# Padding in front of two groups of SBUF tiles, so that matmul operands start at multiples of 2 KB

## The chip, the core and the metric

One NeuronCore of a Trainium2 chip runs the whole program. The metric is the time of one execution on the device in microseconds (us). TensorE (PE in the profile) has two clock levels, 1.2 and 2.4 GHz; the profile gives the granted clock as a share of the upper one. Below, "SBUF address" means the byte offset inside one partition; all 128 partitions of a tile lie at the same offset.

## The reference

One decoder layer over 1,024 tokens of width 1,024, in float32:

```python
h = rmsnorm(x);  proj = h @ w_in                                  # 1024 x 7168
y_a = (a_b * causal_dwconv(a_c * a_x, conv_a_w)) @ w_out_a          # 3 taps
u   = causal_dwconv(c_val * sigmoid(c_gate), conv_b_w) + conv_b_b   # 31 taps
y_b = silu(layernorm(u)) @ w_out_b
x   = x + (sigmoid(gate_a) * y_a + sigmoid(gate_b) * y_b) @ w_o
x   = x + hierarchical_moe(rmsnorm(x))      # 32 experts, top group, top 2 in it, 1024->512->1024
x   = x + sigmoid(rmsnorm(x) @ w_ple_gate) * (p @ w_ple_proj)
return rmsnorm(x)
```

## The kernel before, in words

**Matmul form.** The projections are done in the type float32r (one pass of TensorE). To keep float32 accuracy, both operands are split into a high and a low part (`split`, lines 94 to 96: ACT writes the high part at L95, DVE the low part at L96), and three products are added: high by high, high by low, low by high. Each of them is one instruction on 128 contraction rows, 128 output rows and 512 columns; the trace calls it MATMUL 128x512 f32. The stationary operand (128x128, 512 bytes per partition) is loaded by a LDWEIGHTS of its own for every matmul; the moving operand is 512 columns, 2,048 bytes per partition.

**Stages.**
1. Start (0 to about 43 us): x is normed and transposed into `hT`, the high and low halves of the eight tiles `a0` to `a7` (L143).
2. Loop `s1` (L224 to L253, eight rounds `cb`): five projections of `hT` with chunks of `w_in`. A projection (`proj`, L162) loads a 1024x128 chunk of weights into `wraw` from the SP queue, splits it into the ring tiles `wh` and `wl` (`wchunk`, L146), and issues 48 matmuls at L159: 8 k by 3 products by 2 column halves. DVE also runs the 31-tap convolution here: 30 instructions per round at L251.
3. Block `s2` (L314 to L393): the gates, `w_out_a` and `w_out_b`, again by `proj` and L159; the moving operand is `hT` (tiles a) or `Y` (tiles b), the stationary one again `wh` or `wl`.
4. `w_o` (L419): here the stationary operand is `M`, 128-column slices of the tiles a, and the moving one is the split `w_o` in the tiles b. The routing of the tokens runs beside it.
5. The experts (L830, L857, transposes L794 and L843): plain float32 matmuls. Weights stream from HBM through the same tiles a and b and four more (`c0` to `c3`) with the SP queue.
6. The last stage: the gate matmul with `w_ple_gate`, split as in stage 2 (L1204 for seven blocks of rows, L1271 for the last one). The moving operand is `GW`, in tiles a and b; the stationary one `XW`, 128-column slices of the tiles `xts` and `ys`, filled after transposes (L106).

**Where the tiles lie.** A pool takes a contiguous piece of SBUF when it is opened and places its tiles in it in the order of their first use, each rounded up to a multiple of 32 bytes. `const` comes first, then `big` (the tiles a and b, 8,192 bytes each), then `wrawp` and `wring`, later `mpw` and `mp`. The first tile of `wring` is `vecs`, then `cw`, then the ring `wh`, `wl`. The order of the work is set by the tile framework up to stage 3 and by hand from `w_o` on (`manual_schedule`). The functions that matter here are `layer_kernel`, which holds the pools, and `token_stat`, a helper of stage 3:

Of the kernel before, what the change touches and what calls it, by code (L numbers as in the profile page):

```python
# [10 lines left out]
F32 = mybir.dt.float32  # L11
# [10 lines left out]
T = 1024  # L22
# [41 lines left out]
def layer_kernel(ctx: ExitStack, tc: tile.TileContext, A, out, dbg=None):  # L64
# [3 lines left out]
    const = ctx.enter_context(tc.tile_pool(name="const", bufs=1))  # L68
# [11 lines left out]
    def tpsum():  # L80
        return psum.tile([128, 512], F32, name="tp", bufs=2)
# [4 lines left out]
    def flat(t):  # L86
        return t.rearrange("p a b -> p (a b)")
# [6 lines left out]
    def split(h, l, src):  # L94
        nc.scalar.activation(h, src, AF.Copy)  # L95
        nc.vector.tensor_tensor(l, src, h.bitcast(F32), op=OP.subtract)  # L96

    def rstd_of(dst, ms):

        nc.gpsimd.tensor_scalar(dst, ms, EPS, None, op0=OP.add)  # L100
        nc.gpsimd.tensor_tensor(dst, dst, mhalf[:, :dst.shape[1]], op=OP.pow)
# [17 lines left out]
    def vec(i, k):  # L119
        return vecs[:, i * 8 + k:i * 8 + k + 1]  # L120
# [9 lines left out]
    iota_s = const.tile([1, NE], F32, name="iota_s")  # L130
    ovi = const.tile([1, 2 * NOV + 1], I32, name="ovi")

    big = ctx.enter_context(tc.tile_pool(name="big", bufs=1))
    mix = ctx.enter_context(ExitStack())
    front = mix.enter_context(ExitStack())
    wrawp = front.enter_context(tc.tile_pool(name="wrawp", bufs=3))
    wring = front.enter_context(tc.tile_pool(name="wring", bufs=2))

    vecs = wring.tile([128, NV * 8], F32, name="vecs", bufs=1)
    cw = wring.tile([128, 8, 34], F32, name="cw", bufs=1)  # L140
    bufA = [big.tile([128, 2048], F32R, name=f"a{i}") for i in range(8)]
    bufB = [big.tile([128, 2048], F32R, name=f"b{i}") for i in range(8)]
    hT = [[a[:, i * T:(i + 1) * T] for a in bufA] for i in range(2)]  # L143
# [18 lines left out]
    def proj(src, c0, act):  # L162
        w = wchunk(src, c0)
        ps = mpsum()
        for hf in range(2):
            proj_half(w, ps, act, hf)
        return flat(ps)
# [56 lines left out]
    with tc.tile_pool(name="s1", bufs=2) as s1:  # L224
        for cb in range(8):
            pg = proj(w_in, 4 * D + cb * 128, hT) if cb else flat(fps[0])
            sg = s1.tile([128, T], F32, name="tmp", bufs=2)
            nc.scalar.activation(sg, pg, AF.Sigmoid)
            pv = proj(w_in, 3 * D + cb * 128, hT) if cb else flat(fps[1])
            u = s1.tile([128, KB - 1 + T], F32, name="u")  # L230
            nc.gpsimd.memset(u[:, :KB - 1], 0.0)
            nc.vector.tensor_tensor(u[:, KB - 1:], pv, sg, op=OP.mult)
            acc = s1.tile([128, T], F32, name="acc")
            nc.scalar.activation(acc, u[:, :T], AF.Identity, scale=cw[:, cb, 0:1], bias=vec(V_CB, cb))  # L234
            pc = proj(w_in, D + cb * 128, hT)
            cx = s1.tile([128, T], F32, name="tmp", bufs=2)
            nc.scalar.activation(cx, pc, AF.Copy)
            px = proj(w_in, 2 * D + cb * 128, hT)
            m = s1.tile([128, 2 + T], F32, name="m", bufs=1)
            nc.gpsimd.memset(m[:, :2], 0.0)  # L240
            nc.vector.tensor_tensor(m[:, 2:], px, cx, op=OP.mult)
            c3 = s1.tile([128, T], F32, name="c3", bufs=1)
            nc.scalar.activation(c3, m[:, :T], AF.Copy, scale=cw[:, cb, KB:KB + 1])
            for t in (1, 2):
                nc.vector.scalar_tensor_tensor(c3, m[:, t:t + T], cw[:, cb, KB + t:KB + t + 1], c3,
                                               op0=OP.mult, op1=OP.add)
            pb = proj(w_in, cb * 128, hT)
            nc.vector.tensor_tensor(c3, pb, c3, op=OP.mult)
            split(Y[0][cb], Y[1][cb], c3)
            for t in range(1, KB):  # L250
                nc.vector.scalar_tensor_tensor(acc, u[:, t:t + T], cw[:, cb, t:t + 1], acc,  # L251
                                               op0=OP.mult, op1=OP.add)
            nc.gpsimd.dma_start(u_dram[cb], acc)  # L253
# [59 lines left out]
    with tc.tile_pool(name="s2", bufs=2) as s2:  # L313
        def gate(c0, vi, ob):  # L314
            p = proj(w_in, c0 + ob * 128, hT)
            g = s2.tile([128, T], F32, name="g")
            nc.scalar.activation(g, p, AF.Sigmoid, bias=vec(vi, ob))
            return g

        def token_stat(acc, name):  # L320
            tp = tpsum()
            for tb in range(NT):
                nc.tensor.matmul(tp[:, tb:tb + 1], acc[:, tb * 128:(tb + 1) * 128], ones_col, start=True, stop=True)
            st = s2.tile([128, 8], F32, name=name, bufs=1)
            nc.vector.tensor_scalar(st, tp[:, :8], 1.0 / D, None, op0=OP.mult)
            return st

        def token_bcast(st, name):
            b = s2.tile([128, T], F32, name=name, bufs=1)
            for h in range(2):  # L330
                tp = tpsum()
                for j in range(4):
                    nc.tensor.transpose(tp[:, j * 128:(j + 1) * 128],
                                        st[:, h * 4 + j:h * 4 + j + 1].to_broadcast([128, 128]), ident)
                nc.scalar.activation(b[:, h * 512:(h + 1) * 512], tp, AF.Copy)
            return b

        def u_tile(cb):
            ut = s2.tile([128, T], F32, name="ut", bufs=2)
            nc.scalar.dma_start(ut, u_dram[cb])  # L340
            return ut

        def branch_a(ob):
            g = gate(5 * D, V_GA, ob)
            pa = proj(A["w_out_a"][0], ob * 128, Y)
            ma = s2.tile([128, T], F32, name="ma")
            nc.vector.tensor_tensor(ma, pa, g, op=OP.mult)
            nc.gpsimd.dma_start(mixa_dram[ob], ma)

        stat = s2.tile([128, T], F32, name="stat", bufs=1)  # L350
        for ob in range(4):
            branch_a(ob)
        for cb in range(0, 8):
            ut = u_tile(cb)
            if cb == 0:
                nc.scalar.activation(stat, ut, AF.Copy)
            else:
                nc.vector.tensor_tensor(stat, stat, ut, op=OP.add)
        mub = token_bcast(token_stat(stat, "mu"), "mub")
        for ob in range(4, 8):  # L360
            branch_a(ob)
        for cb in range(8):
            ut = u_tile(cb)
            nc.vector.tensor_tensor(ut, ut, mub, op=OP.subtract)
            if cb == 0:
                nc.scalar.activation(stat, ut, AF.Square)
            else:
                nc.scalar.activation(ut, ut, AF.Square)
                nc.vector.tensor_tensor(stat, stat, ut, op=OP.add)
        rs = token_stat(stat, "var")  # L370
        rstd_of(rs, rs)
        rsb = token_bcast(rs, "rsb")
        for ob in range(8):
            g = gate(6 * D, V_GB, ob)
            nc.gpsimd.dma_start(gb_dram[ob], g)
        S = Y
        for cb in range(8):
            ut = u_tile(cb)
            nc.vector.tensor_tensor(ut, ut, mub, op=OP.subtract)
            nc.vector.tensor_tensor(ut, ut, rsb, op=OP.mult)  # L380
            nc.scalar.activation(ut, ut, AF.Silu, scale=vec(V_LG, cb), bias=vec(V_LB, cb))
            split(S[0][cb], S[1][cb], ut)
        M = [a.rearrange("p (i k t) -> p i k t", i=2, k=KT) for a in bufA]
        for ob in range(8):
            pb = proj(A["w_out_b"][0], ob * 128, S)
            ma = s2.tile([128, T], F32, name="ma")
            nc.scalar.dma_start(ma, mixa_dram[ob])
            g = s2.tile([128, T], F32, name="g")
            nc.scalar.dma_start(g, gb_dram[ob])
            nc.vector.tensor_tensor(g, pb, g, op=OP.mult)  # L390
            nc.vector.tensor_tensor(ma, ma, g, op=OP.add)
            for tb in range(NT):
                split(M[tb][:, 0, ob], M[tb][:, 1, ob], ma[:, tb * 128:(tb + 1) * 128])  # L393
# [918 lines left out]
```

## Time and profile before

| | |
|---|---|
| median of 3 runs | 1678.62 us (1676.21 to 1680.56) |
| the profiled execution | 1680.84 us, span of its instructions 1679.1 us |
| TensorE busy / VectorE / ScalarE / GpSimd | 1595.4 / 815.6 / 351.6 / 171.1 us |
| mean granted TensorE clock | 0.977 |
| HBM read, written | 302.67 MB, 35.11 MB |

The profile is read in the order: which engine is busy in which stage; what the instructions of that stage cost from one start to the next; then which other engine would be the limit there. A duration of a matmul in the trace includes the drain of the array, in which the next matmul already runs. So the rate is read from a stretch of back-to-back matmuls: its length, less the last one's duration, over their number less one; or, in a stretch without a gap, its length over their number.

### The profile page before, as it was taken

How to read it: one execution, taken by the hardware profiler on the slowest of the kernel's cores; microseconds unless marked ns; L12 is line 12 of the kernel's file. 1: busy time of each engine (PE TensorE's matmuls, PEld its weight loads, DVE VectorE, ACT ScalarE, POOL GpSimd, SP SyncE). 2: the span in 40 equal slices, each digit the busy share in tenths (PEclk: the TensorE clock that was granted, in tenths of full speed). 3: DMA queues.
4: the chain of work that ended last, by engine and by line, in shares of the span. 5: the costliest groups of instructions: out<-in, count | busy, mean ns of one | idle time of the engine just before them, and what ended most of it. 6: DMA issues, size and time to landing. Idle time of an engine off the chain costs nothing. (4 is left out here: it accounts for less than half of the span.)

```text
span 1679.1 us, 20527 instructions
## 1 busy us (share of the span) xinstructions
PE 1595.4 (95%) x8112; PEld 1073.1 (64%) x8112; DVE 815.6 (49%) x1113; ACT 351.6 (21%) x533; POOL 171.1 (10%) x318
## 2 busy tenths in 40 slices
PE   6999999999999999999999888999999999799898
PEld 4888888888888888888878642344444443333586
DVE  4888988898883342523454521111111211411575
ACT  4212111211111222732231210100100101011443
POOL 2300000000000000000011221111110201010131
PEclk9999999999999999999999988999999999899899
DMA  5221122112225343434375699999995999899741
GB/s 167 61 63 52 49 63 63 52 50 63 63 68 183 114 127 98 159 107 149 113 276 189 226 332 374 395 384 392 386 389 208 365 358 341 297 352 397 285 163 51
DMA packets 190669, 336.76 MB, mean 201 GB/s; under 512 B 10182, under 2 KB 85022, under 8 KB 190560
## 3 DMA queue, kind: packets, MB, share of 16 engines
q1 hardware_dynamic: 174080, 284.13, 47.7%
q0 software_dynamic: 10576, 29.96, 5.1%
q10 hardware_dynamic: 5904, 21.24, 3.9%
q8 instruction: 66, 1.08, 0.3%
q14 instruction: 43, 0.35, 0.1%
HBM read 302.67 MB, written 35.11 MB: 201 GB/s over the span
## 5 line engine op out<-in xcount | busy, mean ns | idle before, releaser
L159 PE MATMUL mm<-a,wh 128*128 128x512 f32 x1792 | 567.5, 397 | 0.9 <-ACT a L210 0.9
L159 PEld LDWEIGHTS mm<-a,wh 128*128 128x128 f32 x1792 | 337.3, 189 | 82.2 <-ACT a L210 1.5
L159 PE MATMUL mm<-a,wl 128*128 128x512 f32 x896 | 355.0, 396 | 0.0
L251 DVE SCALAR_TENSOR_TENSOR acc<-u,cw,acc 128x1024 f32<-128x1024 f32 x240 | 307.9, 1283 | 7.9 <-ACT acc L234 1.9
L159 PEld LDWEIGHTS mm<-a,wl 128*128 128x128 f32 x896 | 168.7, 188 | 40.0
L95 ACT ACTIVATE wh<-wraw 128x1024 fp32r<-128x1024 f32 x72 | 76.6, 1063 | 523.4 <-PE mm L159 439.9
L159 PE MATMUL mm<-b,wh 128*128 128x512 f32 x512 | 160.9, 396 | 0.0
L830 PE MATMUL p<-a,xts 128*32 128x256 f32 (+2 forms) x600 | 141.5, 524 | 7.2 <-DMA a<-in_w_exp_gate_dram 3.1
L96 DVE TENSOR_TENSOR wl<-wraw,wh 128x1024 fp32r<-128x1024 f32 x72 | 87.8, 1219 | 77.7 <-ACT wh L95 77.6
L868 DVE COPY ys<-p 32x256 f32<-32x256 f32 (+2 forms) x60 | 31.3, 521 | 186.8 <-ACT ys L868 125.4
L830 PE MATMUL p<-b,xts 128*32 128x256 f32 (+2 forms) x528 | 111.0, 462 | 1.6 <-DMA b<-in_w_exp_up_dram 1.6
L159 PEld LDWEIGHTS mm<-b,wh 128*128 128x128 f32 x512 | 96.2, 188 | 23.2
L159 PE MATMUL mm<-b,wl 128*128 128x512 f32 x256 | 101.2, 396 | 0.0
L419 PE MATMUL mm<-b,a 128*128 128x512 f32 x384 | 95.8, 399 | 1.5 <-DVE b L96 1.3
L830 PEld LDWEIGHTS p<-a,xts 128*32 128x32 f32 (+2 forms) x600 | 44.7, 137 | 80.0 <-issue 65.6
L868 ACT COPY ys<-p 32x256 f32<-32x256 f32 (+2 forms) x60 | 26.5, 442 | 328.9 <-PE p L857 328.6
L835 DVE TENSOR_TENSOR hid<-p,hid 64x256 f32<-64x256 f32 (+2 forms) x41 | 22.7, 560 | 128.4 <-ACT hid L834 70.2
L419 PEld LDWEIGHTS mm<-b,a 128*128 128x128 f32 x384 | 69.5, 188 | 16.6 <-DVE b L96 2.4
L844 DVE COPY hT<-h 128x128 f32<-128x128 f32 (+2 forms) x41 | 17.3, 422 | 111.7 <-PE h L843 111.7
L857 PE MATMUL p<-a,hT 128*32 128x256 f32 (+2 forms) x440 | 68.1, 466 | 0.3 <-DVE hT L844 0.3
L830 PEld LDWEIGHTS p<-b,xts 128*32 128x32 f32 (+2 forms) x528 | 39.9, 133 | 43.2 <-issue 35.3
L696 POOL DMA_INDIRECT c<-h_dram,idx x39 | 37.8, 968 | 290.5 <-PE x L794 246.0
(322 smaller groups left out, 1563.2 us busy)
## 6 DMA issues: line engine op xcount, KB each, us to landing
a<-in_w_exp_down_dram SPq DMA_DIRECT2D x32, 1024.0 KB
a<-in_w_exp_gate_dram SPq DMA_DIRECT2D x31, 1024.0 KB
b<-in_w_exp_up_dram SPq DMA_DIRECT2D x30, 1024.0 KB
wraw<-in_w_in_dram SPq DMA_DIRECT2D x56, 512.0 KB
b<-in_w_exp_down_dram SPq DMA_DIRECT2D x28, 1024.0 KB
a<-in_w_exp_up_dram SPq DMA_DIRECT2D x27, 1024.0 KB
b<-in_w_exp_gate_dram SPq DMA_DIRECT2D x24, 1024.0 KB
ut<-u_dram ACTq DMA_DIRECT2D x24, 512.0 KB
```

Of the source, the lines that this page charges most:

```text
L95: nc.scalar.activation(h, src, AF.Copy)
L96: nc.vector.tensor_tensor(l, src, h.bitcast(F32), op=OP.subtract)
L159: nc.tensor.matmul(ps[:, hf], w[wi][:, k], act[ai][k][:, hf * 512:(hf + 1) * 512], start=(k == 0 and i == 0), stop=(k == KT - 1 and i == 2))
L251: nc.vector.scalar_tensor_tensor(acc, u[:, t:t + T], cw[:, cb, t:t + 1], acc, op0=OP.mult, op1=OP.add)
L419: nc.tensor.matmul(ps[-1][:, hf], act(a, k), w(b, k)[:, hf * 512:(hf + 1) * 512], start=(k == 0 and i == 0), stop=(k == nk - 1 and i == 2))
L696: return nc.gpsimd.indirect_dma_start(out=xg, out_offset=None, in_=h2_dram, in_offset=bass.IndirectOffsetOnAxis(ap=ix[:, 0:1], axis=0), bo ...
L830: nc.tensor.matmul(self.gu[j][p:p + r], self.x[:, k], w[:, i:i + self.gu[0].shape[1]], start=(k == 0), stop=(k == KT - 1))
L835: nc.vector.tensor_tensor(self.h, self.gu[1], self.h, op=OP.mult)
L844: nc.vector.tensor_copy(self.hT[:, :4], tp.rearrange("p (f t) -> p f t", f=4))
L857: nc.tensor.matmul(d, self.hT[:, f // 2 + f % 2 * 2 if r == 32 else f], w[:, c * n:(c + 1) * n], start=(f == 0), stop=(f == 3))
L868: (nc.scalar.copy if c < len(self.d) // 2 else nc.vector.tensor_copy)(self.y[:, c * n:(c + 1) * n], d)
```

## The change

Two tiles that nothing reads or writes are added, and two small tiles are made wider; of the wider ones the same columns are used as before. Every instruction stands in the same order on every engine, with the same shapes and the same waits; only addresses differ.

```diff
@@ in layer_kernel, after the last tile of const
     ovi = const.tile([1, 2 * NOV + 1], I32, name="ovi")
+    const.tile([128, 104], F32, name="pad")
     big = ctx.enter_context(tc.tile_pool(name="big", bufs=1))
...
     cw = wring.tile([128, 8, 34], F32, name="cw", bufs=1)
+    wring.tile([128, 184], F32, name="padw", bufs=1)
     bufA = [big.tile([128, 2048], F32R, name=f"a{i}") for i in range(8)]
...
-            m = s1.tile([128, 2 + T], F32, name="m", bufs=1)
+            m = s1.tile([128, 32 + T], F32, name="m", bufs=1)[:, :2 + T]
...
-            st = s2.tile([128, 8], F32, name=name, bufs=1)
+            st = s2.tile([128, 32], F32, name=name, bufs=1)[:, :8]
```

The SBUF addresses of the operands, as the two built programs have them (k counts the 128-row blocks of the contraction, hf the column halves):

| operand | matmuls | before, past a multiple of 2,048 | past a multiple of 512 | after, past a multiple of 2,048 |
|---|---|---|---|---|
| moving: tiles a, b (hT, Y, w_o, GW), + 2,048 hf | all float32r | 1632 | 96 | 0 |
| stationary: `wh`, `wl`, + 512 k | L159 | 896 + 512 k | 384 | 512 k |
| stationary: `M` in tiles a, + 512 k | L419 | 1632 + 512 k | 96 | 512 k |
| stationary: `XW` in `xts`, `ys`, + 512 k | L1204, L1271 | 1632 + 512 k | 96 | 512 k |
| DVE operands `u`, `acc` of L251 | none | 896 or 1024, 1152 | 384 or 0, 128 | 0 or 128, 256 |

The tiles of the transposed tokens (`xt`) in stage 1 and the router's tiles keep their addresses. `wraw`, the experts' weights and `ys` move by 416 bytes, so that the DMA writes into them start at multiples of 2,048 as well.

## Rows read from the trace of the kernel before

**Rows 1.** The page: busy time of PE and DVE, and PE's granted clock by slices.
```profile
PE 1595.4 (95%) x8112; PEld 1073.1 (64%) x8112; DVE 815.6 (49%) x1113; ACT 351.6 (21%) x533; POOL 171.1 (10%) x318
DVE  4888988898883342523454521111111211411575
PEclk9999999999999999999999988999999999899899
```

**Rows 2.** Windows by stage: A:B, length, busy us (instructions) by engine, clock, DMA share, GB/s.
```profile
0.00:43.00 43.00, 27.80 (x128) 20.06 (x129) 20.06 (x29) 20.89 (x33) 10.53 (x58) 1.00 0.53 163
43.00:410.00 367.00, 367.00 (x1580) 295.53 (x1579) 328.25 (x267) 72.03 (x68) 19.83 (x88) 1.00 0.19 58
410.00:841.00 431.00, 431.00 (x1874) 347.88 (x1873) 211.13 (x224) 122.92 (x160) 12.39 (x21) 1.00 0.37 117
841.00:956.00 115.00, 113.23 (x594) 91.74 (x592) 58.98 (x242) 27.52 (x66) 23.76 (x31) 1.00 0.66 227
956.00:1015.00 59.00, 43.87 (x411) 22.15 (x411) 17.98 (x65) 7.35 (x18) 14.52 (x18) 0.81 0.95 324
1015.00:1530.00 515.00, 481.56 (x2792) 200.21 (x2792) 100.53 (x196) 47.76 (x97) 62.67 (x66) 0.96 0.96 355
1530.00:1574.00 44.00, 33.84 (x275) 13.91 (x275) 15.58 (x27) 10.14 (x17) 3.51 (x4) 0.91 0.86 324
1574.00:1679.00 105.00, 97.07 (x468) 81.64 (x468) 63.04 (x67) 42.96 (x74) 23.90 (x32) 0.96 0.41 152
```

**Rows 3.** Groups by line, PE: the four of L159; after the bar busy us, mean ns.
```profile
L159 PE MATMUL mm<-a,wh 128*128 128x512 f32 x1792 | 567.5, 397 | 0.9 <-ACT a L210 0.9
L159 PE MATMUL mm<-a,wl 128*128 128x512 f32 x896 | 355.0, 396 | 0.0
L159 PE MATMUL mm<-b,wh 128*128 128x512 f32 x512 | 160.9, 396 | 0.0
L159 PE MATMUL mm<-b,wl 128*128 128x512 f32 x256 | 101.2, 396 | 0.0
```

**Rows 4.** Windows, PE instructions of L159 alone, in s1 and in s2.
```profile
100.00:400.00 300.00, 300.00 (x1287) 241.70 (x1287) 1.00 0.19 58
460.00:830.00 370.00, 365.52 (x1565) 293.29 (x1564) 1.00 0.40 128
```

**Rows 5.** The chain that ended last, pieces of the last stage: start us, length us, what.
```profile
1608.64 10.90 PE p L1204 x48
1619.54 0.87 PE x L106 x8
1659.88 8.31 PE p L1271 x48
```

**Rows 6.** Timeline of PE: start us, length us, L1204 back to back in the last stage.
```profile
1600.80 5.60 PE L1204 MATMUL p<-a,xts 128*128 128x512 f32 x24
```

**Rows 7.** One line's instructions: L1204, duration ns min/median/max.
```profile
L1204 PE MATMUL p<-a,xts x128: 389/389/775, 1574.7 to 1659.5; 128*128 128x512 f32 x128
```

**Rows 8.** Timeline of PE: the first eleven matmuls of L419.
```profile
841.63 2.66 PE L419 MATMUL mm<-b,a 128*128 128x512 f32 x11
```

**Rows 9.** Windows, PE instructions of L1204, where the granted clock is half.
```profile
1575.30:1579.50 4.20, 4.20 (x11) 0.50 1.03 403
```

**Rows 10.** Timeline of PE: eight matmuls of L1204 in that stretch.
```profile
1575.71 3.62 PE L1204 MATMUL p<-a,xts 128*128 128x512 f32 x8
```

**Rows 11.** The same line in that stretch: duration ns min/median/max.
```profile
L1204 PE MATMUL p<-a,xts x10: 628/628/628, 1575.3 to 1579.1; 128*128 128x512 f32 x10
```

**Rows 12.** Groups by line, DVE, 102 to 400 us; the idle time before them stands last.
```profile
L251 DVE SCALAR_TENSOR_TENSOR acc<-u,cw,acc 128x1024 f32<-128x1024 f32 x160 | 205.3, 1283 | 5.5 <-ACT acc L234 1.4
L232 DVE TENSOR_TENSOR u<-mm,tmp 128x1024 f32<-128x1024 f32 x6 | 7.3, 1224 | 22.7 <-PE mm L159 22.7
L248 DVE TENSOR_TENSOR c<-mm,c 128x1024 f32<-128x1024 f32 x5 | 6.1, 1225 | 2.9 <-PE mm L159 2.9
```

**Rows 13.** One line's instructions, 102 to 400 us: L251, duration ns min/median/max.
```profile
L251 DVE SCALAR_TENSOR_TENSOR acc<-u,cw,acc x160: 1274/1285/1287, 101.6 to 399.9; 128x1024 f32<-128x1024 f32 x160
```

## The prediction, made before the changed kernel ran

> **What bounds the kernel now.** I read the page first, then the table of stages, then the rate of the matmuls in each stage. TensorE is busy for 95% of the span, VectorE for 49% [rows 1]. By stage [rows 2] that splits: from 43 to 841 us TensorE is busy in every microsecond at full clock with a DMA share of 0.19 to 0.37, so there the matmul rate alone sets the end; 841 to 956 us is much the same (113.23 of 115). From 1015 to 1530 us the DMA engines are busy at a share of 0.96 (355 GB/s), while TensorE has 481.56 of 515 us: the stream of expert weights sets that end. The last stage is TensorE again; the chain that ended last runs through L1204 and L1271 [rows 5].
>
> The matmuls of 43 to 841 us are those of L159: 1792 + 896 + 512 + 256 = 3,456 [rows 3]. Their rate: 1,287 touch a stretch of 300 us without a gap [rows 4], two of them cut by its ends, so 300 / 1,286 = 233.3 ns from start to start. At 2.4 GHz, 512 columns at one per clock are 213.3 ns, so **20.0 ns are lost per matmul**. The same instruction elsewhere loses less:
> - L1204 in the last stage: (5.60 - 0.39) / 23 = 226.5 ns [rows 6, 7], a loss of 13.2.
> - L419, first eleven: (2.66 - 0.39) / 10 = 227 ns [rows 8]; later ones are interrupted by transposes.
> - L1271: 24 matmuls of 512 and 24 of 256 columns take 8.31 us [rows 5]; their columns alone would take 24 x (213.3 + 106.7) = 7.68 us, so 13.1 ns are lost per matmul, whatever its width.
>
> Two rows say what kind of loss it is. At the lower clock (0.50, [rows 9]) L1204 runs at (3.62 - 0.63) / 7 = 427 ns [rows 10, 11], and 512 / 1.2 GHz is 426.7: no loss. And the float32 transposes of 128 columns take 0.87 / 8 = 108.8 ns [rows 5], which is two clocks per column (106.7) and 2.1 ns. So the loss appears only where an operand is fed at one column per 2.4 GHz clock. That points at reading SBUF, not at issue.
>
> L159 and the other three lines have the same shape, type and kind of PSUM output. What differs is the address of the stationary operand. The moving one lies at 96 past a multiple of 512 everywhere; the stationary one at 96 too for L419, L1204 and L1271, at 384 for L159. Which multiple of 512 it is (k steps through four of them per 2 KB, across a 2 KB boundary) shows nowhere: the four groups of L159 have means of 396 to 397 ns [rows 3].
>
> **The change, part by part.** No instruction is added, removed or moved, so every term is a rate.
>
> *L159.* After the change the moving operand starts at 0 and the stationary one at a multiple of 512: the distance between them is a multiple of 512, as in the three faster lines before. I take their rate, 226.5 ns. Some of the 3,456 matmuls run in the first 43 us, between transposes, where TensorE holds only 128 instructions of all lines [rows 2]; I leave out 56. Then 3,400 x (233.3 - 226.5) = 3,400 x 6.8 = **-23 us**. The bounds: nothing, if the distance does not matter; below, the loss of the float32 rows, 2.1 ns, so 215.4 ns and 3,400 x 17.9 = -61 us; above, one more step of the size seen between the two kinds of lines, 3,400 x 6.8 = +23 us. I take the inner value because its row has the same instruction and the same distance.
>
> *L419, L1204, L1271.* 384 + 336 + 72 = 792 matmuls keep their distance; I take 0. Bounds: to 215.4 ns, 792 x 11.1 = -9 us; one step up, 792 x 6.8 = +5 us.
>
> *What stands behind TensorE in s1.* A round has 240 matmuls, 240 x 233.3 = 56.0 us. DVE waits for TensorE at L232 and L248 for 22.7 + 2.9 us in 298 us [rows 12], that is 5.3 rounds, so 4.8 us per round: DVE needs 51.2. At 226.5 ns a round of TensorE is 54.4 us, at 215.4 it is 51.7. DVE stays just below in both, so it takes nothing away, but below 51.2 / 240 = 213 ns it would. Its own operands move as well; the 30 taps of L251 start 4 bytes apart each, and they all cost 1274 to 1287 ns [rows 13], so I put the new addresses of DVE and ACT operands at 0.
>
> *The transfers.* Destinations move by 416 bytes. Before 841 us they are hidden (share 0.19 to 0.37 [rows 2]); in the experts' stage they set the end, but no row separates destinations of two kinds: 0, with 1% of 515 us either way, 5 us, as a bound that I chose.
>
> *What is late next.* The experts' loads are released by the rows of L419, so the whole later part shifts with the end of L159: nothing takes the saving back there.
>
> Sum: 1680.84 - 23 = 1657.8 for the profiled execution, which lies 2.2 us above the median of the runs; so **1656 us** against 1678.6.
>
> One rule speaks against the change. The rows show two rates for one instruction at two addresses, 233.3 and 226.5 ns. The Trainium skill, TensorE: Matmul & The Clock Gate, section Step-by-step: what each phase is for, says that the moving operand and the weight load have independent read ports, so that loading the next weights takes nothing from the running matmul. By that rule the sum would be 0 and the time 1678.6; it leaves the difference of the two rates unexplained.
>
> **The rivals.**
> - *The start itself counts, for the moving operand too.* All float32r matmuls, those at the good distance included, lose 13 ns, and before the change every moving operand starts at 1632; no row shows another start. If a start on a boundary removes the loss, L159 goes to 215.4 ns and the other lines with it: -61 - 9 = -70, 1609 us; if it removes half of the 13 ns, L159 runs at 220 and the rest too: 3,400 x 13.3 + 792 x 6.5 = -50, 1628 us. For it: the loss is the same for 256 and 512 columns, as something at the start of each would be. Against: nothing yet. [...]
> - *The change does nothing:* 1679 us. Then the two rates come from something that goes along with the line: L159 reads weights that were split only some microseconds before, through a ring, L1204 operands as fresh. For it: L159 is the only one of these lines that reads from a ring. Against: the rate is the same in s1, where DVE is nearly full, and in s2, where it is not [rows 2, 4]. The skill's rule on the ports, above, gives this time as well.
> - *Alignment is what costs.* L159's stationary operand lies at a multiple of 128 bytes before (896 + 512 k), those of the faster lines do not (1632 + 512 k), and it is the aligned one that is slower. If reads that start on a common boundary meet, L419, L1204 and L1271 take the slow rate: 792 x 6.8 = +5, 1684 us; if the moving operand's alignment adds a step of its own, L159 goes to 240.1 ns: +23 + 5, 1707 us. It decides from L159 at 233.3 + 5 / 3,400 x 1000 = 234.8 ns on. For it: the order of the two rates as it stands. Against: the fast lines have both operands on the same phase of 512 bytes, which is where a meeting should be worst.
>
> **How the numbers follow.** About 0.3%, 5 us, is what a measurement of this kernel can tell from no change. Chances: the forecast 0.36 (own range 1650 to 1662), the start itself 0.28, nothing 0.22, alignment costs 0.14. Faster by over 0.3% is the first two, 0.64; within it 0.22; slower 0.14. The time is that of the likeliest. The range runs from the full gain to no change with the spread of the runs, **1608 to 1682 us**; left out are the slower case and the edges, about 0.2.
>
> **What would show it.** The windows over L159 alone: 300 us should hold 1,325 matmuls (226.5 ns) instead of 1,286; 1,393 would be the full gain, 1,286 no effect, under 1,278 the slower rival. The chain's piece of L1204 with 48 matmuls should still take 10.9 us; 10.3 would say that the start counts. DVE's wait before L232 should shrink from 4.3 us a round to about 2.8. The experts' stage should keep its length and shift. The prediction is wrong if L159's rate does not move, or if L1204's moves as well.

## The result, and the profile after

The changed kernel takes 1649.3 us (median of 4 runs, 1647.4 to 1653.7) against 1679.5 for the kernel before; the ratio is 0.9834, 95% interval 0.9815 to 0.9853, so it is faster by 1.5 to 1.9%. The forecast was 1656, with 1650 to 1662 for its own mechanism. The profiled execution took 1647.99 us, its span is 1646.2. (Every source line below the padding stands three lines lower: L159 is now L162, L419 L422, L1204 L1207, L1271 L1274, L251 L254, L232 L235.)

The page of the kernel after, busy times:

```profile
PE 1561.0 (95%) x8112; PEld 1068.9 (65%) x8112; DVE 814.4 (49%) x1113; ACT 351.3 (21%) x533; POOL 170.9 (10%) x318
```

TensorE is busy for 34.4 us less with the same 8,112 matmuls [rows 1]. The table of stages, with the boundaries where the kernel after has them:

```profile
43.00:410.00 367.00, 367.00 (x1625) 303.66 (x1624) 337.34 (x276) 73.93 (x70) 19.77 (x89) 1.00 0.20 59
410.00:818.00 408.00, 408.00 (x1825) 338.37 (x1824) 200.32 (x215) 120.47 (x158) 12.29 (x20) 1.00 0.38 122
...
994.00:1499.00 505.00, 471.93 (x2778) 197.98 (x2778) 100.38 (x196) 47.77 (x97) 62.67 (x66) 0.97 0.94 359
```

In the same 367 us from 43 to 410, TensorE now gets through 1,625 instructions instead of 1,580 [rows 2]. The experts' stage changed as well: the 16 DMA engines were busy for a share of 0.96 of the time at 355 GB/s, and now for 0.94 at 359.

The window of L162 alone, and two of its four groups by line:

```profile
100.00:390.00 290.00, 290.00 (x1281) 240.19 (x1280) 1.00 0.19 59
```

```profile
L162 PE MATMUL mm<-a,wh 128*128 128x512 f32 x1792 | 556.1, 391 | 0.9 <-ACT a L213 0.9
L162 PE MATMUL mm<-b,wh 128*128 128x512 f32 x512 | 157.6, 389 | 0.0
```

The rate is 290 / 1,280 = 226.6 ns, from 233.3 [rows 4], and the mean durations of these two groups have come down to 391 and 389 ns; 389 is the median that L1204 had all along [rows 3, 7]. The chain in the last stage is as before [rows 5]:

```profile
1564.04 10.90 PE p L1207 x48
...
1627.01 8.31 PE p L1274 x48
```

These pieces moved their operands without changing the distance and take the same time, to the hundredth of a us. And VectorE, in s1:

```profile
L235 DVE TENSOR_TENSOR u<-mm,tmp 128x1024 f32<-128x1024 f32 x6 | 7.3, 1224 | 17.2 <-PE mm L162 17.2
L251 DVE TENSOR_TENSOR c<-mm,c 128x1024 f32<-128x1024 f32 x5 | 6.1, 1217 | 0.0
```

Its waits for TensorE shrank from 22.7 + 2.9 us [rows 12] to 17.2, so it is not yet the limit.

Where the time went can be read from the first and last starts of three lines. These two rows are from the views of single lines of the kernel after:

```profile
L422 PE MATMUL mm<-b,a x384: 387/389/505, 818.4 to 934.5; 128*128 128x512 f32 x192
```

```profile
L1207 PE MATMUL p<-a,xts x128: 387/389/775, 1543.7 to 1626.6; 128*128 128x512 f32 x128
```

This table is made from such rows, for all kernels of this study that do the whole layer; those below "after" are described under The experiments. Each time in it is that of one profiled execution, each ratio is against runs of the kernel before that were taken beside that kernel. "To w_o" ends with the last L159, "w_o" with the last L419, "experts" with the first L1204, "last" with the span. The multiple of 256 is that of the large tiles (and so of the destinations of the weights); the distance is the stationary start of L159 less its moving one. The rate is a stretch over a count of matmuls, so it is good to one in 1,280, 0.2 ns.

| kernel | large tiles at a multiple of 256 | distance mod 256 | L159, ns | to w_o | w_o | experts | last | ratio to before, 95% |
|---|---|---|---|---|---|---|---|---|
| before | no | 32 | 233.3 | 840.9 | 114.4 | 619.4 | 104.4 | |
| after | yes (2,048) | 0 | 226.6 | 818.2 | 116.3 | 609.2 | 102.5 | 0.9815 to 0.9853 |
| ring_only | no | 0 | 226.4 | 817.5 | 115.7 | 618.5 | 104.5 | 0.9836 to 0.9870 |
| pad_only | yes (2,048) | 32 | 233.1 | 840.8 | 115.8 | 611.3 | 102.5 | 0.9948 to 0.9978 |
| pad32 | no (128) | 32 | 233.3 | 840.2 | 114.7 | 618.2 | 104.5 | 0.9992 to 1.0013 |
| pad512 | yes (512) | 32 | 233.1 | 839.6 | 115.6 | 610.2 | 102.6 | 0.9934 to 0.9969 |
| pad256 | yes (256) | 32 | 233.1 | 840.0 | 118.1 | 608.2 | 104.2 | 0.9918 to 0.9963 |
| pads256 | yes (256) | 0 | 226.4 | 817.9 | 115.8 | 608.6 | 104.3 | 0.9792 to 0.9827 |

Of the 32.9 us between the two spans, 22.7 were won in the matmuls of L159, as forecast. The experts' stage gave another 10.2, which the forecast had at 0; the last stage gave 1.9 and w_o took 1.9 back.

### The profile page after: what moved, and what is told of

Read it like the earlier page. It is cut to its first block, busy times and chain, and to the rows that moved or that the text cites. A ratio compares the mean times of both kernels' runs of the same rounds, so it can differ in the third digit from the quotient of the medians.

```text
span 1646.2 us, 20527 instructions
## 1 busy us (share of the span) xinstructions
PE 1561.0 (95%) x8112; PEld 1068.9 (65%) x8112; DVE 814.4 (49%) x1113; ACT 351.3 (21%) x533; POOL 170.9 (10%) x318
## 5 line engine op out<-in xcount | busy, mean ns | idle before, releaser
L162 PE MATMUL mm<-a,wh 128*128 128x512 f32 x1792 | 556.1, 391 | 0.9 <-ACT a L213 0.9
L162 PEld LDWEIGHTS mm<-a,wh 128*128 128x128 f32 x1792 | 336.9, 188 | 71.3 <-ACT a L213 1.5
L162 PE MATMUL mm<-a,wl 128*128 128x512 f32 x896 | 349.4, 390 | 0.0
L254 DVE SCALAR_TENSOR_TENSOR acc<-u,cw,acc 128x1024 f32<-128x1024 f32 x240 | 307.9, 1283 | 7.9 <-ACT acc L237 1.9
L162 PEld LDWEIGHTS mm<-a,wl 128*128 128x128 f32 x896 | 168.5, 188 | 34.4
L162 PE MATMUL mm<-b,wh 128*128 128x512 f32 x512 | 157.6, 389 | 0.0
L162 PEld LDWEIGHTS mm<-b,wh 128*128 128x128 f32 x512 | 96.1, 188 | 19.9
L162 PE MATMUL mm<-b,wl 128*128 128x512 f32 x256 | 99.6, 389 | 0.0
L422 PE MATMUL mm<-b,a 128*128 128x512 f32 x384 | 95.8, 399 | 1.3 <-DVE b L96 1.3
L838 DVE TENSOR_TENSOR hid<-p,hid 64x256 f32<-64x256 f32 (+2 forms) x41 | 22.7, 560 | 119.4 <-ACT hid L837 62.6
L422 PEld LDWEIGHTS mm<-b,a 128*128 128x128 f32 x384 | 69.6, 188 | 16.3 <-DVE b L96 2.1
## 6 DMA issues: line engine op xcount, KB each, us to landing
a<-in_w_exp_down_dram SPq DMA_DIRECT2D x32, 1024.0 KB, 13.3
```

What stands on the lines that cost most here:

```text
L162: nc.tensor.matmul(ps[:, hf], w[wi][:, k], act[ai][k][:, hf * 512:(hf + 1) * 512], start=(k == 0 and i == 0), stop=(k == KT - 1 and i == 2))
L422: nc.tensor.matmul(ps[-1][:, hf], act(a, k), w(b, k)[:, hf * 512:(hf + 1) * 512], start=(k == 0 and i == 0), stop=(k == nk - 1 and i == 2))
L838: nc.vector.tensor_tensor(self.h, self.gu[1], self.h, op=OP.mult)
```

## The experiments

Two questions: is it the distance of the two operands that sets the rate (theory D), or the starts themselves (S), or a common boundary that costs (C)? And did the experts' stage gain from the addresses (A) or is that variation (V)?

**One half of the change at a time.** The ring's padding alone:

```diff
     cw = wring.tile([128, 8, 34], F32, name="cw", bufs=1)
+    wring.tile([128, 184], F32, name="padw", bufs=1)
```

> The 736 bytes in front of the weights' ring alone: moving operand and ring both at 1632 past a multiple of 2 KB, nothing aligned, distance 0. Theory D: L159 at 226.7 ns, 23 us gained in 43 to 841 us. Theory S and rival C: L159 stays at 233.3 ns, no gain. On the 7 us that the change gained beyond the forecast: theory A (aligned destinations make the DMA packets of the expert weights cheaper) expects none of it here, so 1656 us; theory V (it is only variation between executions and chips) expects 1649 to 1656.

1653.4 us, ratio 0.9853 (0.9836 to 0.9870). L159 (here L160) in its window, and a window over the experts:

```profile
100.00:390.00 290.00, 290.00 (x1282) 240.14 (x1280) 1.00 0.19 59
```

```profile
933.00:1507.00 574.00, 524.11 (x3196) 222.01 (x3194) 118.66 (x261) 55.12 (x115) 77.22 (x84) 0.95 0.96 353
```

290 / 1,281 = 226.4 ns with nothing aligned at all: both operands start at 1632 past a multiple of 2 KB. So alignment to 2 KB plays no part in the rate, which goes against S and C. The experts' stage stays at 618.5 us, with a share of 0.96 for 353 GB/s. The like window of the kernel before is

```profile
955.00:1530.00 575.00, 526.13 (x3207) 222.59 (x3205) 118.77 (x261) 55.11 (x115) 77.19 (x84) 0.95 0.96 352
```

The total, 1653.4 us, lies inside what V allowed and 2.6 us below A's 1656, so it does not decide; the length of the stage is what speaks for A.

The other half, the padding in front of the large tiles alone:

```diff
     ovi = const.tile([1, 2 * NOV + 1], I32, name="ovi")
+    const.tile([128, 104], F32, name="pad")
```

> The 416 bytes in front of the large tiles alone: moving operand and the destinations of the expert weights at multiples of 2 KB, ring at 1312 past one, distance still 288. Theory D: L159 stays at 233.3 ns. Theory S: the moving start is aligned, so L159 at 226.7 ns or less and L1204 faster than 226.5. Theory A: the experts' stage becomes some 8 us shorter, 1671 us in all, with 84 instead of 87 ns for a packet of 2 KB. Theory V: 1679 us, packets at 87 ns.

1671.7 us, ratio 0.9963 (0.9948 to 0.9978). The same two windows:

```profile
100.00:400.00 300.00, 300.00 (x1288) 241.70 (x1287) 1.00 0.19 58
```

```profile
957.00:1523.00 566.00, 517.35 (x3185) 220.89 (x3189) 118.68 (x261) 55.13 (x115) 77.20 (x84) 0.95 0.94 356
```

L159 is as slow as before (300 / 1,287 = 233.1 ns) although its moving operand is aligned, and the experts' stage is 8 us shorter, with a share of 0.94 for 356 GB/s. In that stage (1015 to 1500 us) the median packet of 2 KB takes 84 ns, against 87 in the same stretch of the kernel before and of ring_only, as A expected. The two halves are two separate effects (neither has the two widened tiles of the change): 0.9853 x 0.9963 = 0.9817, within the interval of the whole change.

**The rate of a matmul against its two addresses.** A kernel of matmuls alone, with the loop that matters:

```diff
+    for mo in range(0, 128, 8):        # moving start, in floats
+        for so in range(0, 128, 8):    # stationary start
+            ...
+            for i in range(N):         # N = 32
+                m0, s0 = mo + i % 2 * 512, so + i % 4 * 128
+                nc.tensor.matmul(ps, sv[:, s0:s0 + 128], mv[:, m0:m0 + 512], start=(i == 0), stop=(i == N - 1))
```

> This kernel leaves the whole layer out: it writes x to the output and runs only float32r matmuls of 128x512, 32 in a row for each of 16 x 16 starts of the moving and the stationary operand (0 to 480 bytes past a multiple of 512, in steps of 32), then 16 starts of the stationary operand in bf16, then 16 in float32r with 256 columns. Theory D (distance): the rate depends only on the difference of the two starts modulo 512, so all 16 pairs on a diagonal agree; difference 0 gives 226.7 ns, difference 288 gives 233.3, whatever the moving start. Theory S (the start itself): the rate depends on the moving start; with it at 0 the loss goes and 216 ns appear. Rival C (common boundary): pairs in which both starts are multiples of 128 are the slow ones, over 233 ns. For bf16 all theories expect 216 ns with no dependence, as fewer bytes are read per clock; for 256 columns theory D expects 120 ns at difference 0 and 127 at 288.

Its timeline (start us, length us, what) for the moving operand at 0, with the stationary one at 0, 32, 64 and so on; the PSUM tiles e and o alternate, so each pair of starts has a row:

```profile
17.86 7.42 PE L50 MATMUL o<-mv,sv 128*128 128x512 f32 x32
25.12 7.62 PE L50 MATMUL e<-mv,sv 128*128 128x512 f32 x32
32.58 7.63 PE L50 MATMUL o<-mv,sv 128*128 128x512 f32 x32
40.05 7.64 PE L50 MATMUL e<-mv,sv 128*128 128x512 f32 x32
47.53 7.59 PE L50 MATMUL o<-mv,sv 128*128 128x512 f32 x32
54.96 7.63 PE L50 MATMUL e<-mv,sv 128*128 128x512 f32 x32
62.42 7.49 PE L50 MATMUL o<-mv,sv 128*128 128x512 f32 x32
69.75 7.63 PE L50 MATMUL e<-mv,sv 128*128 128x512 f32 x32
77.22 7.42 PE L50 MATMUL o<-mv,sv 128*128 128x512 f32 x32
84.48 7.62 PE L50 MATMUL e<-mv,sv 128*128 128x512 f32 x32
...
396.32 7.42 PE L50 MATMUL e<-mv,sv 128*128 128x512 f32 x32
403.58 7.62 PE L50 MATMUL o<-mv,sv 128*128 128x512 f32 x32
...
1917.58 7.08 PE L56 MATMUL o<-mb,sb 128*128 128x512 bf16 x32
1924.50 7.07 PE L56 MATMUL e<-mb,sb 128*128 128x512 bf16 x32
...
2027.91 4.18 PE L62 MATMUL o<-mv,sv 128*128 128x256 f32 x32
2031.93 3.95 PE L62 MATMUL e<-mv,sv 128*128 128x256 f32 x32
2035.71 3.94 PE L62 MATMUL o<-mv,sv 128*128 128x256 f32 x32
```

From one start to the next, over 32: distance 0 is (25.12 - 17.86) / 32 = 226.9 ns, distance 32 is 233.1, and from the eighth step on, at distance 256, it begins again with (84.48 - 77.22) / 32 = 226.9. The row at 396.32 us has both operands at 96: (403.58 - 396.32) / 32 = 226.9 again, at distance 0. Over the whole grid, from the middle of each 32 to the start of the next row, all pairs of the same distance modulo 256 agree within 1.4 ns:

| distance mod 256 | 0 | 32 | 64 | 96 | 128 | 160 | 192 | 224 |
|---|---|---|---|---|---|---|---|---|
| ns from start to start, mean | 227.2 | 233.2 | 233.4 | 234.0 | 232.5 | 233.2 | 229.3 | 233.2 |

For starts at multiples of 32 bytes, as all tiles of the layer have them, theory D holds, with a period of 256, not of 512 bytes. Distance 288, that of the kernel before, is 32 here. A common boundary does not cost: both at 0 and both at 96 are equally fast. Two expectations came out otherwise. Nothing in the row of moving start 0 reached 216 ns, which S wanted. And with 256 columns the bad distance does not cost: 0 takes 120.0 ns in the steady state (the first row here still has its start in it) and 32 takes (2035.71 - 2031.93) / 32 = 118.1, where D had 120 and 127; the 16 starts lie between 117.3 and 120.0. In bf16 all 16 starts of the stationary operand, with the moving one at a single start, take 215.8 to 215.9 ns in the steady state.

**Is there a better distance between the steps of 32 bytes?** The same kernel with other ranges:

```diff
-    for mo in range(0, 128, 8):
-        for so in range(0, 128, 8):
+    for mo in (0, 1, 2, 4):
+        for so in range(64):
```

> This kernel leaves the whole layer out: it writes x to the output and runs float32r matmuls of 128x512, 32 in a row, with the stationary operand 0 to 252 bytes past a multiple of 512 in steps of 4 and the moving one at 0, 4, 8 and 16 bytes. The grid before showed the rate to depend on the distance of the two starts modulo 256 in steps of 32. [...] Rival: at some distance off the multiples of 32 the loss goes, 216 ns, and a version faster by 3,400 x 11 = 37 us could be made.

Rows with the moving operand at 0 and the stationary one at 0, 4, 100 and 104 bytes, then with the moving one at 4 and the stationary one at 0, 4 and 8:

```profile
18.52 7.42 PE L50 MATMUL o<-mv,sv 128*128 128x512 f32 x32
25.78 7.60 PE L50 MATMUL e<-mv,sv 128*128 128x512 f32 x32
...
204.65 7.42 PE L50 MATMUL e<-mv,sv 128*128 128x512 f32 x32
211.91 7.62 PE L50 MATMUL o<-mv,sv 128*128 128x512 f32 x32
...
493.87 7.73 PE L50 MATMUL o<-mv,sv 128*128 128x512 f32 x32
501.44 7.63 PE L50 MATMUL e<-mv,sv 128*128 128x512 f32 x32
508.91 7.65 PE L50 MATMUL o<-mv,sv 128*128 128x512 f32 x32
```

From one start to the next, none of the 256 pairs is under 226.8 ns; the dearest is 240.9. With the moving operand at 4 bytes every pair lies above that floor, at 231 to 241 ns; the first row here takes (501.44 - 493.87) / 32 = 236.6. So no start that was tried, here or in the grid, takes away the 11 ns that are left over the bf16 rate.

The same rows bound theory D. Off the multiples of 32 the distance alone does not set the rate: at distance 0 it is 226.9 ns with both operands at 0, but (508.91 - 501.44) / 32 = 233.4 with both at 4, and 231.2 and 231.1 with both at 8 and at 16. And other distances reach the floor there: with the moving operand at 0, the stationary one at 100 takes (211.91 - 204.65) / 32 = 226.9, and 120, 132, 144, 156, 228 and 252 run at 226.7 in the steady state. These runs show no rule for such starts.

**The transfers by themselves.** A kernel that streams expert weights into six tiles at a given start, no engine computing:

```diff
+STARTS = (0, 32, 128, 256, 512, 1024, 1632, 0)      # bytes past a multiple of 2 KB
...
+        for g, o in enumerate(STARTS):
+            for i in range(N):                        # N = 16
+                t = into[i % 6][:, o // 4:o // 4 + 2048]...
+                ...
+                nc.sync.dma_start(t, src[e % 32, r * rows:(r + 1) * rows, :]...)
```

> This kernel leaves the whole layer out: it writes x to the output and streams expert weights into SBUF, no engine computing: 16 transfers of 1 MB each in packets of 2 KB at starts of 0, 32, 128, 256, 512, 1024, 1632 and again 0 bytes past a multiple of 2 KB, then the same in packets of 4 KB. Theory A1 (the start alone makes a packet dear): the groups at 32, 128 and 1632 have some 87 ns per packet of 2 KB and 3% less GB/s than the first and the last group with 84 ns. Theory A2 (packets get dear only beside engines that use SBUF, or beside other transfers): all groups at 84 and 159 ns, the same GB/s within 1%.

Windows inside the groups (length, POOL busy, clock, DMA share, GB/s), packets of 2 KB at 0, 32, 128, 256, 512, 1024, 1632 and 0, then of 4 KB at 32 and 256:

```profile
0.00:44.00 44.00, 0.20 (x4) 1.00 0.98 376
45.00:87.00 42.00, 0.00 (x0) 1.00 1.04 389
88.00:131.00 43.00, 0.00 (x0) 1.00 1.05 387
132.00:172.00 40.00, 0.00 (x0) 1.00 1.05 408
173.00:213.00 40.00, 0.00 (x0) 1.00 1.05 409
214.00:254.00 40.00, 0.00 (x0) 1.00 1.05 409
255.00:297.00 42.00, 0.00 (x0) 1.00 1.05 388
298.00:338.00 40.00, 0.00 (x0) 1.00 1.05 409
```

```profile
379.00:419.00 40.00, 0.00 (x0) 1.00 1.02 411
...
461.00:500.00 39.00, 0.00 (x0) 1.00 1.02 421
```

Destinations at 32, 128 and 1632 get 387 to 389 GB/s, those at a multiple of 256 get 408 to 409, that is 5% more at the same share (the first window holds the start of the program). From share and rate, a packet of 2 KB takes 1.05 x 16 x 2,048 B / 409 GB/s = 84 ns of an engine against 88. In packets of 4 KB the loss is half as large, 411 against 421 GB/s. Theory A1 holds: the start of the destination alone makes the packets dearer. The trace has a duration for each packet: with destinations at 256 (132 to 172 us) every packet of 2 KB takes 84 ns; at 32 (45 to 87 us) a quarter of them take no more than that, and nearly all others 85 to 96, most often 88.

**Which boundary the layer needs.** 32, 160 and 928 bytes in front of the large tiles instead of 416:

```diff
+    const.tile([128, 8], F32, name="pad")      # pad32: 128 past a multiple of 256
+    const.tile([128, 40], F32, name="pad")     # pad256
+    const.tile([128, 232], F32, name="pad")    # pad512
```

> Only 32 bytes in front of the large tiles: moving operand and destinations at 1664 past a multiple of 2 KB, which is a multiple of 64 and 128; ring at 928, distance still 288. Theory D: L159 at 233.3 ns. Theory A: if a boundary of 64 or 128 bytes is what the packets need, the experts' stage is some 8 us shorter, 1671 us; if 2 KB is needed, 1679 us. Theory V: 1679 us.

> 160 bytes in front of the large tiles: they start at 1792 past a multiple of 2 KB, a multiple of 256; distance as before. Theory D: L159 at 233.3 ns. Theory A: with a multiple of 256 enough, the experts' stage at 609 to 611 us and the time 1672; if 512 or 2 KB is needed, 618 and 1678.

> 928 bytes in front of the large tiles: they start at 512 past a multiple of 2 KB; the distance of L159's operands stays at 32 modulo 256. Theory D: L159 at 233.3 ns. Theory A: if a multiple of 512 is enough for the packets, the experts' stage is as short as with both 2 KB kernels (609 to 611 us from the last matmul of w_o to the first of the last stage, against 618 to 619) and the time 1672; if a row of 2 KB must not cross a multiple of 2 KB, 618 and 1678.

Windows over the experts of the three, in this order:

```profile
955.00:1528.00 573.00, 525.11 (x3202) 223.09 (x3201) 118.69 (x261) 55.12 (x115) 77.22 (x84) 0.94 0.96 353
```

```profile
958.00:1521.00 563.00, 515.30 (x3184) 219.83 (x3182) 118.61 (x261) 55.21 (x115) 77.40 (x84) 0.96 0.94 358
```

```profile
955.00:1520.00 565.00, 518.07 (x3184) 221.42 (x3182) 118.67 (x261) 55.13 (x115) 77.22 (x84) 0.95 0.94 357
```

pad32 takes 1679.3 us (ratio 1.0003, 0.9992 to 1.0013), pad256 1671.6 (0.9941), pad512 1671.8 (0.9952). A multiple of 128 does nothing that these runs can tell, and a multiple of 256 as much as 2 KB. In all three L159 keeps its 233 ns, since the distance stayed at 32 modulo 256.

**The least that does both.**

```diff
+    const.tile([128, 40], F32, name="pad")
...
+    wring.tile([128, 120], F32, name="padw", bufs=1)
```

> The smallest padding that the runs so far call for: 160 bytes in front of the large tiles (1792 past a multiple of 2 KB, a multiple of 256) and 480 in front of the ring, so that the distance of L159's operands is 256 modulo 512, that is 0 modulo 256. Theory D with a period of 256 and theory A1 with a boundary of 256 together: L159 at 226.7 ns, the experts' stage at 608 to 611 us, 1649 us, as the change itself. If 2 KB, or distance 0 modulo 512, adds anything: L159 at 233.3 ns (1672 us), or 1652 to 1656.

1646.5 us, ratio 0.9810 (0.9792 to 0.9827), its interval overlaps that of the change. The window of L159 (here L161), whose operands now lie 256 modulo 512 apart, gives 290 / 1,281 = 226.4 ns; the experts' stage takes 608.6 us:

```profile
100.00:390.00 290.00, 290.00 (x1282) 240.19 (x1281) 1.00 0.19 59
```

640 bytes per partition do what the change does with 1,152 in its two new tiles, and neither the large tiles nor `wh` and `wl` start at a multiple of 2 KB. The two widened tiles of the change are not needed either.

## Why the prediction was right, and which term was off

The stated range, 1608 to 1682 us, holds the times of two rivals as well, so the time alone says little. What speaks for the mechanism is the rate of L159 and where the time was won.

- *What bounds each stage.* Right. The saving in L159 came through whole: the last of its matmuls moved from 840.9 to 818.2 us.
- *L159.* Forecast 226.5 ns and -23 us; measured 226.6 and -22.7. The reason given, that the distance of the two operands counts, is shown by the grid and by ring_only for starts at multiples of 32 bytes; the period I read into it, 512 bytes, was too long: it is 256. That the loss is the same whatever the width was read from L1271, at distance 0, and the grid agrees there: 226.7 less 213.3 and 120.0 less 106.7 are both 13.3 ns. At other distances it does not hold: at 32, 512 columns lose 20 ns and 256 columns 12.
- *L419, L1204, L1271.* Forecast no change. The pieces of L1204 and L1271 in the chain are the same to 0.01 us, and the first eleven matmuls of L419 start 227 ns apart before and 226.7 after.
- *VectorE in s1.* Right: 17.2 us of waiting are left in 298 us, 3.1 per round of 54.4; the forecast was 2.8.
- *The transfers.* This is the term that was mis-sized: I put it at 0, with 5 us either way as a bound of my own choosing, since no row of the kernel before has destinations of two kinds. It measured 10.2 us in the experts' stage of the profiled executions, twice that bound; for the whole kernel pad_only gives 0.9963, some 6 us. The sentence that the experts' stage should keep its length and shift was wrong with it. The forecast missed the median by 6.7 us, about this much, which put the time just below the 1650 to 1662 of its own mechanism.
- *The last stage and w_o.* 1.9 us less and 1.9 more. The former lies in the first piece of L1207, 42 matmuls in 10.08 us where before they took 11.84: the granted clock is 0.50 there at first [rows 9], for 5.1 us of the line before and for 1.3 us after. pad256 and pads256, whose destinations start at multiples of 256 too, have 104.2 and 104.3 us, so it is not an effect of the addresses that these runs can show. w_o varies between 114.4 and 116.3 us over seven kernels; pad256 has 118.1, with 3.5 us at a granted clock of 0.51 (858 to 861 us). Why the rest varies stays open.
- *The rivals.* The start itself (0.28), as put, falls: no start reaches 216 ns in float32r, and at multiples of 32 the moving start makes no difference at a given distance. That the change does nothing (0.22) falls with L159 at 226.6 ns. The Trainium skill, TensorE: Matmul & The Clock Gate, section Step-by-step: what each phase is for, says that loading weights takes nothing from the running matmul. For float32r that does not hold here: with the same moving operand a matmul takes 226.9 or 233.1 ns, by where its weights are read. For bf16 no run contradicts it: 215.8 ns at all 16 starts. Alignment that costs (0.14) falls too: both operands at a multiple of 512 are among the fastest pairs.

What happens when the two reads are at a bad distance is not shown; only that the rate depends on it, in float32r with 512 columns at a granted clock of 1.00. At the lower clock the bad distance costs nothing: here are matmuls of L159 in the kernel before, back to back at its start (start us, length us, what).

```profile
21.16 0.63 PE L159 MATMUL mm<-a,wh 128*128 128x512 f32 x1
21.59 0.63 PE L159 MATMUL mm<-a,wl 128*128 128x512 f32 x1
22.01 1.47 PE L159 MATMUL mm<-a,wh 128*128 128x512 f32 x3
```

They start 426 to 427 ns apart, as L1204 does at the good distance with a clock of 0.50 [rows 10, 11], and the first four last 628 ns, the duration that it has there; the record of the clock itself begins after them, at 23.3 us.

## What to carry to other kernels

Where float32r matmuls of 512 columns run back to back, place both on multiples of 32 bytes and the stationary tiles so that their starts differ from the moving ones' by a multiple of 256 bytes: that was worth 6.7 ns of 233 each here, for one unused tile. Where a stage is bound by loads, start the destinations at a multiple of 256 bytes, which gave 5% more GB/s in packets of 2 KB and 2% in packets of 4 KB with the transfers alone, and 8 to 11 us of 619 in the experts' stage. Two lines with the same instruction and different rates in one profile are worth asking about; the addresses are not in the trace and have to be worked out from the pools.

## What was not expected of the hardware

- A matmul's rate depends on where its two operands lie: 226.8 to 240.9 ns for the same float32r instruction of 512 columns, at multiples of 32 bytes by their distance modulo 256; in bf16 16 starts of the stationary operand made no difference (215.8 ns).
- DMA packets into SBUF cost 88 instead of 84 ns per 2 KB in the mean when the destination is 32, 128 or 1632 bytes past a multiple of 2 KB and not at a multiple of 256; a multiple of 128 is no better than one of 32 (387 and 389 GB/s).
